# Hybrid decoder layer on one core: the first product in four row pieces and the front in a pinned order

## The chip, the cores and the metric

The kernel runs on one core of one Trainium2 chip. The metric is the device time of one execution in microseconds (us), from several runs of the same program; lower is better. The core has five engines that work side by side: PE (TensorE, matmuls and transposes), DVE (VectorE), ACT (ScalarE), POOL (GpSimd) and SP (SyncE, which here only issues loads). Each runs its own list of instructions in order and waits on the others by semaphores. SP, ACT and POOL also issue DMA transfers, each from its own queue.

## The reference

One decoder layer for 512 tokens of width 1024: a token mixer that adds attention with compressed, selected and windowed keys to a gated recurrence, then a mixture of 16 experts, then a gated per-layer embedding. The change touches the very beginning, where the input is normalised and multiplied with the first columns of `w_in`:

```python
def rmsnorm(x, g):
    xf = x.astype(jnp.float32)
    y = xf * lax.rsqrt(jnp.mean(xf * xf, axis=-1, keepdims=True) + EPS)
    return (y * g.astype(jnp.float32)).astype(x.dtype)
...
        h = rmsnorm(x, g_mix[i])
        z = h @ w_in[i]
        (q_a, kc_a, vc_a, ks_a, vs_a, kw_a, vw_a, gate_a, qk_b, v_b, o_b, if_b, merge) = jnp.split(z, offs, axis=-1)
        nsa_q = partial_rope(q_a.reshape(b, s, NSA_HEADS, NSA_HD), cos, sin)
        k_cmp = partial_rope(kc_a.reshape(b, s, NSA_KV, NSA_HD), cos, sin)
        k_sel = partial_rope(ks_a.reshape(b, s, NSA_KV, NSA_HD), cos, sin)
...
def compress_blocks(tok_g, w1, w2, pe):
...
    blk = tok_g[:, :, idx] + pe
    flat = blk.reshape(b, g, n_cmp, CMP_LEN * d)
    return jax.nn.gelu(flat @ w1) @ w2
```

Columns 0 to 511 of `z` are the queries, 512 to 639 the keys and 640 to 767 the values that are compressed (`kc_a`, `vc_a`), 768 to 1023 keys and values of the selected branch, 1024 to 1279 those of the window. `w_ck1` and `w_cv1` are the two `w1` of the compression, 2048 rows of 256 columns each; `w_ck2`, `w_cv2` the two `w2`.

## The kernel before

**Numbers in two parts.** Every 32-bit factor is split into a hi (rounded to the matmul's format) and a low (the value less its hi), and each product is three matmuls: hi by hi, low by hi, hi by low. For a weight the class `Stream` does this piece by piece: `_load` issues the load of a raw piece on SP (line 77; pool `WR`, four buffers), `_split` makes the hi on ACT (line 103) and the low on DVE (line 106) or on POOL (line 108) from column `pool_from` on. A piece is 128 partitions by 1024 numbers or somewhat less. `get(key)` gives a piece's two parts, loading and splitting in the order of the list.

**Order of the first products.** `ORDER` lists them: `z2` and `z3` are columns 512 to 767 and 768 to 1023, each in two pieces of 256 columns by half of the rows; `z4` is three pieces of 288 columns (1024 to 1303 and eight gate columns), `c0` and `c1` are four pieces each of `w_ck1` and `w_cv1`, and `z0`, `z1` the queries. `z1_mm` and `tok_mm` (matmuls on line 271) run a `z` piece for the four blocks of 128 tokens; `cmp_mm` (line 589) a `c` piece. `z1_out` turns a finished product into what later stages read, partly in generators that `begin` and `advance` call between the matmuls of later pieces.

**The front**, from line 299 on: x is loaded in four blocks (block 0 in two halves, by SP and ACT), and for each block ACT squares and sums it (lines 364 and 390), DVE makes the scale factor (`rstd`, from line 217; `rstd_cols` for blocks 2 and 3 together, from line 231), DVE multiplies it with the factor and the gain (line 372), PE transposes it in eight pieces (line 376), ACT makes the hi `hTh` (line 383) and DVE the low `hTl` (line 385). The gain row is spread over 128 partitions by two matmuls with a row of ones into `gmb` (line 320). Fourteen transposes of an identity, `keep_warm`, are issued there too (line 264). `tok_mm_late` (line 282) runs z2's product for block 0 in an order fit to when its parts come. `angles` (lines 321 to 351) makes the tables of sine and cosine from the positions. Seven small loads fill `rows` (lines 398 to 401), which PE transposes to `cols` (lines 438 to 440). What is not tied by `issue_after` (`after`) is put in order by a scheduler from the data dependences.

**Behind the front.** `finish_c2` transposes the rotated keys (`zt`) and the values (line 526) into `TT`; `cmp_in` adds the position terms into `tb` (line 580) and makes `bhl`, hi (line 581) and low (line 582), which all `c` matmuls read. `w2s` is loaded on POOL (lines 566 and 567) and copied to `w2d` on DVE (line 569). For z3 and z4, `v` (line 547) is the low of the values; it is the last to read an accumulator. The accumulators are in three `mm` and two `S` tiles of PSUM, and transposes go to two `tp`.

## Time and profile before

| | us |
|---|---|
| three runs: median (lowest to highest) | 709.09 (708.98 to 711.17) |
| the profiled execution, its own time | 711.02 |
| its span | 709.3 |
| around the span | 1.72 |
| PE busy, share of the span | 684.3, 96% |
| DVE busy, share of the span | 563.2, 79% |
| ACT busy, share of the span | 436.0, 61% |
| POOL busy, share of the span | 130.4, 18% |

The profile is of one execution, whose own time stands 1.93 above the median of the three runs. Times in it count from the start of the span. An instruction is named by its line, engine and operation, and then by what it writes and reads: `mm<-whWS,hTl` is a matmul into the tile `mm` of a weight's hi by the low of the normalised input. "Idle before" is how long the engine stood before it, and what ended that. Matmuls overlap, so the pace of PE is read from the distance between two starts. "PEclk" is the TensorE clock that was granted, where 1.00 is full speed.

### The profile page before, as it was taken

How to read it: one execution, taken by the hardware profiler on the slowest of the kernel's cores; microseconds unless marked ns; L12 is line 12 of the kernel's file. 1: busy time of each engine (PE TensorE's matmuls, PEld its weight loads, DVE VectorE, ACT ScalarE, POOL GpSimd, SP SyncE). 2: the span in 40 equal slices, each digit the busy share in tenths (PEclk: the TensorE clock that was granted, in tenths of full speed). 3: DMA queues.
4: the chain of work that ended last, by engine and by line, in shares of the span. 5: the costliest groups of instructions: out<-in, count | busy, mean ns of one | idle time of the engine just before them, and what ended most of it. 6: DMA issues, size and time to landing. Idle time of an engine off the chain costs nothing.

```text
span 709.3 us, 11568 instructions
## 1 busy us (share of the span) xinstructions
PE 684.3 (96%) x3913; PEld 584.6 (82%) x3913; DVE 563.2 (79%) x1427; ACT 436.0 (61%) x848; POOL 130.4 (18%) x184
## 2 busy tenths in 40 slices
PE   7989989999999999999999999999999999999995
PEld 5989976889999998888888888876788888887784
DVE  5877989888777758888884673668999999986986
ACT  6447746576666666665553332326999999986642
POOL 5010023333334220000000001222222222110000
PEclk9999999999999999999999999999999999999998
DMA  8424551222121212332219438944999999607511
GB/s 267 124 73 140 167 140 32 85 65 61 31 60 30 61 31 64 87 79 71 83 38 354 146 119 266 375 154 157 388 394 362 355 329 365 245 31 269 191 63 60
DMA packets 83152, 113.72 MB, mean 160 GB/s; under 512 B 9553, under 2 KB 52129, under 8 KB 83090
## 3 DMA queue, kind: packets, MB, share of 16 engines
...
## 4 chain that ended last, share of the span: by engine, by line
PE 79%; DVE 8%; DMA 6%; ACT 4%; issue 2%; POOL 1%; ACTq 0%; POOLq 0%; DVEq 0%
PE mm L945 12%; PE S L1476 11%; PE mm L271 10%; PE mm L1648 6%; PE mm L1501 6%; PE mm L1117 6%; PE mm L768 3%; PE mm L1281 3%; PE S L271 2%; PE tp L862 2%; DMA wr<-in_w_re 2%; PE S L841 2%; PE tp L1462 2%; DVE wlWS L106 1%; ACT whWS L103 1%
## 5 line engine op out<-in xcount | busy, mean ns | idle before, releaser
L106 DVE TENSOR_TENSOR wlWS<-rawWR,whWS 128x1024 fp32r<-128x1024 f32 (+2 forms) x78 | 89.5, 1153 | 28.6 <-ACT whWS L103 27.5
L103 ACT ACTIVATE whWS<-rawWR 128x1024 fp32r<-128x1024 f32 (+2 forms) x79 | 82.3, 1050 | 43.0 <-PE S L271 8.5
L106 DVE TENSOR_TENSOR wlWS<-rawWE,whWS 128x1024 fp32r<-128x1024 f32 x58 | 69.1, 1221 | 3.7 <-ACT whWS L103 2.4
L103 ACT ACTIVATE whWS<-rawWE 128x1024 fp32r<-128x1024 f32 x58 | 60.6, 1071 | 5.1 <-PE S L1476 4.5
L271 PE MATMUL mm<-whWS,hTl 128*128 128x256 f32 (+1 forms) x200 | 59.3, 296 | 1.4 <-DVE hTl L385 1.4
L271 PE MATMUL mm<-wlWS,hTh 128*128 128x256 f32 (+1 forms) x200 | 59.1, 296 | 0.0
L271 PE MATMUL mm<-whWS,hTh 128*128 128x256 f32 (+1 forms) x200 | 59.1, 296 | 0.0
L945 PE MATMUL mm<-hTh,whWS 128*128 128x512 f32 x128 | 50.3, 393 | 0.0
L945 PE MATMUL mm<-hTh,wlWS 128*128 128x512 f32 x128 | 50.0, 391 | 0.0
L945 PE MATMUL mm<-hTl,whWS 128*128 128x512 f32 x128 | 50.0, 391 | 0.0
L852 POOL TENSOR_SCALAR pr<-pr,sm 128x128 f32<-128x128 f32 (+3 forms) x64 | 35.2, 564 | 78.1 <-DVE sm L850 36.4
L1476 PE MATMUL S<-whWS,tgh 128*128 128x512 f32 x120 | 48.6, 405 | 0.0
L1476 PE MATMUL S<-wlWS,tgh 128*128 128x512 f32 x120 | 47.8, 398 | 0.1
L1476 PE MATMUL S<-whWS,tgl 128*128 128x512 f32 x120 | 47.3, 394 | 0.0
L846 ACT ACTIVATE pr<-pr,sm 128x128 f32<-128x128 f32 (+3 forms) x64 | 35.4, 555 | 16.9 <-DVE sm L844 16.8
L271 PEld LDWEIGHTS mm<-whWS,hTl 128*128 128x128 f32 x200 | 38.6, 193 | 1.7 <-DVE hTl L385 1.6
L271 PEld LDWEIGHTS mm<-wlWS,hTh 128*128 128x128 f32 x200 | 38.6, 193 | 0.0
L271 PEld LDWEIGHTS mm<-whWS,hTh 128*128 128x128 f32 x200 | 38.5, 193 | 0.1
L108 POOL TENSOR_TENSOR wlWS<-rawWR,whWS 128x384 fp32r<-128x384 f32 (+1 forms) x17 | 24.8, 1460 | 72.4 <-ACT whWS L103 67.5
L865 ACT ACTIVATE ph<-tp 128x512 fp32r<-128x512 f32 (+1 forms) x48 | 25.1, 523 | 20.4 <-PE tp L862 20.1
L842 DVE CUSTOM_DVE_ANT_0 pr<-S,strip 128x128 f32<-128x128 f32 (+3 forms) x64 | 29.3, 485 | 3.9 <-PE S L841 3.4
...
## 6 DMA issues: line engine op xcount, KB each, us to landing
rawWE<-in_w_e SPq DMA_DIRECT2D x59, 512.0 KB, 9.9
rawWR<-in_w_in SPq DMA_DIRECT2D x40, 512.0 KB, 3.9
mT<-in_w_e SPq DMA_DIRECT2D x22, 512.0 KB, 12.6
rawWR<-in_w_e SPq DMA_DIRECT2D x13, 512.0 KB, 10.4
rawWR<-in_w_out SPq DMA_DIRECT2D x8, 512.0 KB, 4.3
yy<-y_dram SPq DMA_DIRECT2D x8, 512.0 KB, 5.4
rawWR<-in_w_ck SPq DMA_DIRECT2D x4, 512.0 KB, 3.9
rawWR<-in_w_cv SPq DMA_DIRECT2D x4, 512.0 KB, 5.4
```

What stands on the lines that cost most here:

```text
L103: self.last_hi = self.nc.scalar.activation(h[:, :n], flat, AF.Copy)
L106: self.last = self.nc.vector.tensor_tensor(l[:, :c], flat[:, :c], h[:, :c].bitcast(F32), OP.subtract)
L271: T.matmul(dst[b], a[:, kk, b * P:(b + 1) * P], w[:, kk - k0, :n], start=(kk == 0 and i == 0 and b % share == 0), stop=(kk == NK - 1 and i ...
L842: V.tensor_tensor_reduce(pr[:, hh, :n], s_[:, :n], strip[:, 512 - q0:640], 0.125, -3.0e38, OP.add, OP.max, sm[:, 0, hh:hh + 1])
L846: A.activation(pr[:, hh, :n], pr[:, hh, :n], AF.Exp, bias=sm[:, 1, hh:hh + 1], accum_out=sm[:, 2, hh:hh + 1])
L852: G.tensor_scalar(pr[:, hh, :n], pr[:, hh, :n], sm[:, 3, hh:hh + 1], 1.0, op0=OP.mult, op1=OP.mult)
L865: A.activation(ph[:, :nj], tp[:, :nj], AF.Copy)
L945: T.matmul(ps, w[:, k], a[:, k], start=(k == 0 and i == 0), stop=(k == NK - 1 and i == 2))
L1117: T.matmul(ps, w[:, k, f * P:(f + 1) * P], a[:, k], start=(k == 0 and i == 0), stop=(k == 3 and i == 2))
L1476: T.matmul(ps, a[:, 2 * m + k], w[:, k], start=(m == 0 and k == 0 and i == 0), stop=(m == 3 and k == 1 and i == 2))
L1501: T.matmul(acc[c], a[:, k], w[:, 0, c * 512:(c + 1) * 512], start=(k == 0 and i == 0), stop=(k == 1 and i == 2))
L1648: T.matmul(acc, a[:, k], w[:, 0, lo:hi], start=(k == 0 and i == 0), stop=(k == NK - 1 and i == 2))
```

## The change

Columns 512 to 1023 become one product of 512 columns, in four pieces of 256 rows each (`zz`, m = 0 to 3), whose hi and low have a pool of their own (`W0`, four pairs). `zz_mm` runs two k-tiles of a block and some of the three terms, into four accumulators `accz`, one for each block of tokens. The orders of all engines inside the front are pinned by `in_order`, which ties every instruction to the one before it on its engine, in the order of the code:

- all four lows, and the lows of the first two z4 pieces, go to POOL (`pool_from` = 0);
- ten keep-warm transposes stand ahead of the gain matmuls, and these write `mm` and `o`;
- the gain row is loaded by SP in second place, the positions by ACT, and the b_if row, which ACT loaded at the start, comes last of eight small loads on POOL, behind the four lows;
- the positions are cast on POOL and copied from PSUM on ACT; `angles` is in two parts;
- of block 0's squares, the first half is ACT's, the second a `scalar_tensor_tensor` of DVE with a sum;
- z4's first two pieces are fetched inside the front, with accumulators `mm`, `mm`, `mm`, `S`;
- `finish_c2` and z3's outputs are begun ahead of the list, one block pair after the other, and two memsets on POOL stay behind the front.

The diff, cut to what the prediction speaks of:

```diff
-N_WARM = 14
+N_WARM = 10
-ORDER = "z2 z2 z3 z3 z4 z4 c0 z4 c0 c0 z0 c0 z0 c1 z1 c1 z1 c1 c1".split()
+ORDER = "z4 z4 c0 z4 c0 c0 z0 c0 z0 c1 z1 c1 z1 c1 c1".split()
...
+    for m in range(4):
+        st.add(("zz", m), [(0, 512, wall[:, 2 * m:2 * m + 2, 512:1024])], [P, 2, 512], first[0], split_from("W0"))
...
+    def in_order():
...
+            if i.engine in last:
+                tc.add_manual_dep(i, last[i.engine].name, mybir.DependencyInfo(
+                    mybir.DependencyClass.NoSync, mybir.DependencyReason.DATA), reason="in_order")
+            last[i.engine] = i
...
+    def zz_mm(b, m, terms):
+
+        wh, wl = zw[m]
         for i in terms:
             a, w = ((hTh, wh), (hTl, wh), (hTh, wl))[i]
+            for kk in range(2):
+                last = T.matmul(accz[b], a[:, 2 * m + kk, b * P:(b + 1) * P], w[:, kk], start=(m == 0 and i == 0 and kk == 0),
+                                stop=(m == 3 and i == 2 and kk == 1), skip_group_check=True)
+        return last
...
+        st.pool_from = st.split_ahead = 0
+        with in_order():
+            for b in range(NB):
+                t = sp.tile([P, D], F32, name="xs", bufs=NB)
+                if b == 0:
+                    nc.sync.dma_start(t[:, 0:512], x[0, 0:P, 0:512])
+                    A.dma_start(t[:, 512:D], x[0, 0:P, 512:D])
+                    nc.sync.dma_start(grow, g_mix)
+                    A.dma_start(posr, positions[0].rearrange("(a b) -> a b", b=P))
+                else:
+                    nc.sync.dma_start(t, x[0, b * P:(b + 1) * P])
+                xs.append(t)
+                if b < 2:
+                    st._load()
+                    st._load()
...
+            G.tensor_copy(posf, posr)
+            keep_warm(N_WARM)
+
+            gmb = [PM.tile([P, 512], F32, name="mm"), PO.tile([P, 512], F32, name="o")]
+            for c in range(2):
+                T.matmul(gmb[c], ones, grow[:, c * 512:(c + 1) * 512], start=True, stop=True)
+            tpp = PA.tile([P, 512], F32, name="tp")
+            T.transpose(tpp[:, :NB], posf, ident[:NB, :NB])
+            junk0 = [sp.tile([P, 512], F32, name="junk0", bufs=2) for _ in range(2)]
+            A.activation(junk0[0], xs[0][:, 0:512], AF.Square, accum_out=ss[:, 0:1])
+            V.scalar_tensor_tensor(junk0[1], xs[0][:, 512:D], 1.0, xs[0][:, 512:D], op0=OP.mult, op1=OP.mult,
+                                   accum_out=ss[:, 1:2])
+            A.activation(pos, tpp[:, :NB], AF.Copy)
+            V.tensor_tensor(ss[:, 0:1], ss[:, 0:1], ss[:, 1:2], OP.add)
+            rstd(rst[:, 0:1], ss[:, 0:1], sp)
+            for m in range(2):
+                zw.append(st.get(("zz", m)))
+            scaled(0)
+            ps = turned(0)
+            angles_1()
+            square(1)
+            highs(0, ps)
+            rstd(rst[:, 1:2], ss[:, 1:2], sp)
+            lows(0, ps)
+            for m in range(2, 4):
+                zw.append(st.get(("zz", m)))
+            for m, i in ((0, 0), (1, 0), (0, 2), (1, 2), (0, 1), (1, 1), (2, 0), (2, 1), (2, 2), (3, 0), (3, 1)):
+                zz_mm(0, m, (i,))
+            scaled(1)
+            ps = turned(1)
+            zz_mm(0, 3, (2,))
+            square(2)
+            highs(1, ps)
+            square(3)
+            lows(1, ps)
+            rstd_cols(rst[:, 2:4], ss[:, 2:4], sp, 2)
+            scaled(2)
+            scaled(3)
...
+            last_g = nc.gpsimd.dma_start(bif, bass.AP(tensor=b_if.tensor, offset=b_if.offset, ap=[[0, P], [1, 8]]))
+            z4w = [st.get(("z", 4, 0))]
...
-    bif = const.tile([P, 8], F32, name="bif")
-    A.dma_start(bif, bass.AP(tensor=b_if.tensor, offset=b_if.offset, ap=[[0, P], [1, 8]]))
```

`scaled`, `turned`, `highs` and `lows` are the four steps of a block (multiply on DVE, eight transposes on PE, hi on ACT, low on DVE); `turned` is on line 347 of the changed kernel, `zz_mm` on 304.

What the pinned order moves is read from the two programs' lists of instructions, with the line numbers of each kernel.

**ACT, from the first square to block 0's highs.** `junk` is the square, `whWS` and `whW_176`, `whW_183`, `whW_222`, `whW_228` are the hi parts of weight pieces, `pos` the copy of the transposed positions. Before:

```order
5 L390 ACTIVATE junk_136,ss<-xs 128x512
6 L390 ACTIVATE junk_138,ss<-xs 128x512
7 L103 ACTIVATE whWS<-rawWR 128x1024
8 L364 ACTIVATE junk,ss<-xs 128x1024
9 L383 ACTIVATE hTh<-tp 128x4x128 x2
10 L97 ACTIVATE whWS<-rawWR 128x1024
```

With the change:

```order
4 L411 ACTIVATE junk_161,ss<-xs 128x512
5 L414 ACTIVATE pos<-tp 128x4
6 L103 ACTIVATE whW_176<-rawWR 128x1024
7 L103 ACTIVATE whW_183<-rawWR 128x1024
8 L337 ACTIVATE junk,ss<-xs 128x1024
9 L355 ACTIVATE hTh<-tp 128x4x128 x2
10 L103 ACTIVATE whW_222<-rawWR 128x1024
11 L103 ACTIVATE whW_228<-rawWR 128x1024
```

The second half of the square is gone, the copy of `pos` stands ahead of the first hi, two hi stand ahead of block 1's square, and two more come between block 0's highs and the next square.

**POOL, around the small loads.** `wlWS` and `wlW_...` are low parts of weight pieces. Before:

```order
13 L257 AFFINE_SELECT cany<-cany 128x1
14 L108 TENSOR_TENSOR wlWS<-rawWR,whWS 128x1024
15 L398 DMA rows<-in_g_ple 8x128
16 L398 DMA rows<-in_b_conv 8x128
17 L398 DMA rows<-in_g_hn 4x128
18 L398 DMA rows<-in_g_ffn 8x128
19 L399 DMA rows<-in_w_conv 32x128
20 L400 DMA rows<-in_pe_ck 16x128
21 L401 DMA rows<-in_pe_cv 16x128
22 L461 MEMSET strip 128x640
23 L470 MEMSET vcm 128x1024
```

With the change:

```order
14 L108 TENSOR_TENSOR wlW_177<-rawWR,whW_176 128x1024
15 L108 TENSOR_TENSOR wlW_184<-rawWR,whW_183 128x1024
16 L108 TENSOR_TENSOR wlW_223<-rawWR,whW_222 128x1024
17 L108 TENSOR_TENSOR wlW_229<-rawWR,whW_228 128x1024
18 L441 DMA rows<-in_g_ple 8x128
19 L441 DMA rows<-in_b_conv 8x128
20 L441 DMA rows<-in_g_hn 4x128
21 L441 DMA rows<-in_g_ffn 8x128
22 L442 DMA rows<-in_w_conv 32x128
23 L443 DMA rows<-in_pe_ck 16x128
24 L444 DMA rows<-in_pe_cv 16x128
25 L445 DMA bif<-in_b_if 128x8
```

Three more whole lows stand ahead of the loads of `rows`, the load of `bif` is behind them, and two lows of z4 pieces come ahead of the rest.

**DVE, around the copy of `w2d`.** `v_425` and `v_454` are the values of the selected branch (z3), `zt` and `kz` the rotated keys. Before:

```order
67 L482 TENSOR_TENSOR zt<-rope_a,rope_b 128x2x2x16
68 L569 COPY w2d<-w2s 128x256
69 L106 TENSOR_TENSOR wlWS<-rawWR,whWS 128x1024
70 L547 TENSOR_TENSOR v_425<-S,v_425 128x2x64
71 L478 TENSOR_TENSOR rope_a<-kz,trig 128x2x2x8
72 L479 TENSOR_TENSOR rope_a<-kz,trig 128x2x2x8
73 L547 TENSOR_TENSOR v_425<-S,v_425 128x2x64
```

With the change:

```order
67 L510 TENSOR_TENSOR rope_a<-zt,trig 128x2x2x8
68 L511 TENSOR_TENSOR rope_a<-zt,trig 128x2x2x8
69 L514 TENSOR_TENSOR kz<-rope_a,rope_b 128x4x16
70 L601 COPY w2d<-w2s 128x256
71 L512 TENSOR_TENSOR rope_b<-zt,trig 128x2x2x8
72 L513 TENSOR_TENSOR rope_b<-zt,trig 128x2x2x8
73 L579 TENSOR_TENSOR v_454<-S,v_454 128x2x64
74 L584 TENSOR_TENSOR qs<-kz,qs 128x2x2x64
75 L514 TENSOR_TENSOR zt<-rope_a,rope_b 128x2x2x16
76 L579 TENSOR_TENSOR v_454<-S,v_454 128x2x64
```

The copy of `w2d` stood behind both rotations of `zt` and ahead of a weight's low; now it stands between two halves of the second rotation, ahead of the `v_454` that read the accumulator `S`.

## Rows read from the trace of the kernel before

**Rows 1.** The page, busy time of each engine over the whole span.

```profile
PE 684.3 (96%) x3913; PEld 584.6 (82%) x3913; DVE 563.2 (79%) x1427; ACT 436.0 (61%) x848; POOL 130.4 (18%) x184
```

**Rows 2.** Chain of waits, 0 to 110 us: start us, us, what.

```profile
34.23 4.42 DMA w2s<-in_w_ck
...
45.41 2.02 DVE tb L580 x2
```

**Rows 3.** PE's timeline, 0 to 23 us: start us, us, engine, line, operation.

```profile
4.44 3.75 PE L320 MATMUL S<-grow,ones 1*128 1x512 f32 x4 [4.44 <-DMA grow<-in_g_mix]
8.12 3.25 PE L264 MATMUL o<-ident 128*128 128x128 f32 x14
...
15.23 1.03 PE L376 MATMUL tp<-ident,xs 128*128 128x128 f32 x8
...
18.51 0.38 PE L271 MATMUL mm<-whWS,hTl 128*128 128x256 f32 x1 [1.40 <-DVE hTl L385]
```

**Rows 4.** PE's timeline, 40.5 to 52 us.

```profile
41.01 1.03 PE L526 MATMUL tp<-ident,zt 128*128 128x128 f32 x8
...
47.90 0.37 PE L271 MATMUL S<-whWS,hTh 128*128 128x288 f32 x1 [2.00 <-DVE v L547]
48.11 0.29 PE L271 MATMUL S<-whWS,hTl 128*128 128x288 f32 x1
48.24 0.30 PE L271 MATMUL S<-wlWS,hTh 128*128 128x288 f32 x1
...
49.23 0.44 PE L271 MATMUL S<-wlWS,hTh 128*128 128x288 f32 x1
49.47 0.44 PE L271 MATMUL mm<-wlWS,hTh 128*128 128x288 f32 x1
```

**Rows 5.** One window: stretch and us, busy by engine, PEclk, DMA share, GB/s.

```profile
50.00:52.00 2.00, 2.00 (x10) 2.00 (x10) 2.00 (x3) 0.52 (x1) 0.00 (x0) 0.50 0.00 0
```

**Rows 6.** PE's timeline at 68 us.

```profile
68.00 0.28 PE L589 MATMUL o<-wlWS,bhl 128*128 128x256 f32 x1
68.12 0.28 PE L589 MATMUL o<-whWS,bhl 128*128 128x256 f32 x1
```

**Rows 7.** Chain of waits, 255 to 330 us: matmuls of 512 columns.

```profile
270.21 2.74 PE mm L945 x12
```

**Rows 8.** ACT's timeline and queue, 0 to 23 us.

```profile
1.81 0.36 ACTq L695 DMA_DIRECT2D bif<-in_b_if  x1
...
4.20 0.63 ACT L390 ACTIVATE junk<-xs 128x512 f32<-128x512 f32 x1 [0.71 <-DMA xs<-in_x]
...
5.72 1.06 ACT L103 ACTIVATE whWS<-rawWR 128x1024 fp32r<-128x1024 f32 x1
```

**Rows 9.** DMA issues of 0 to 3 us: tile, queue, count, KB each, us to landing.

```profile
xs<-in_x SPq DMA_DIRECT2D x2, 512.0 KB, 7.7
...
posr<-in_positions POOLq DMA_DIRECT2D x1, 2.0 KB, 6.9
```

**Rows 10.** POOL's timeline, 0 to 102 us.

```profile
6.86 2.35 POOL L108 TENSOR_TENSOR wlWS<-rawWR,whWS 128x1024 fp32r<-128x1024 f32 x1 [4.17 <-ACT whWS L103]
9.17 0.56 POOL L398 DMA_DIRECT2D rows<-in_g_ple  x1
...
90.59 2.62 POOL L108 TENSOR_TENSOR wlWS<-rawWR,whWS 128x384 fp32r<-128x384 f32 x2 [36.52 <-ACT whWS L103]
```

**Rows 11.** DVE's timeline, 0 to 101 us.

```profile
7.72 1.41 DVE L372 SCALAR_TENSOR_TENSOR xs<-xs,rst,S 128x512 f32<-128x512 f32 x2
...
91.28 1.05 DVE L478 TENSOR_TENSOR rope_a<-zt,trig 128x64 f32<-128x64 f32 x1
...
93.21 0.21 DVE L480 TENSOR_TENSOR rope_b<-zt,trig 128x64 f32<-128x64 f32 x1
```

**Rows 12.** DVE's timeline, 43 to 50 us.

```profile
43.51 0.75 DVE L534 COPY TT<-tp 64x256 f32<-64x256 f32 x2
...
44.61 0.77 DVE L534 COPY TT<-tp 64x256 f32<-64x256 f32 x2
...
48.59 1.19 DVE L582 TENSOR_TENSOR bhl<-tb,bhl 128x992 fp32r<-128x992 f32 x1 [0.17 <-ACT bhl L581]
```

**Rows 13.** The low on POOL, all of line 108: ns shortest, middle, longest.

```profile
L108 POOL TENSOR_TENSOR wlWS<-rawWR,whWS x17: 997/1642/2352, 6.9 to 228.3; 128x384 fp32r<-128x384 f32 x16, 128x1024 fp32r<-128x1024 f32 x1
```

More of the change, by code (lines that the diff above doesn't have):

```diff
@@ L263, in keep_warm @@
         for _ in range(n):
-            T.transpose(warm[:, 0:P], ident, ident)
+            last = T.transpose(warm[:, 0:P], ident, ident)
+        return last
     def tok_mm_steps(dst, k0, k1, wh, wl, n, share, blocks=range(NB)):
@@ L316, in tile_hybrid @@
[L316 to L332 removed]
+        posf = sp.tile([NB, P], F32, name="posf")
@@ new lines, in scaled, with turned, part @@
+        def scaled(b):
+            for c in range(2):
+                sl = slice(c * 512, (c + 1) * 512)
+                V.scalar_tensor_tensor(xs[b][:, sl], xs[b][:, sl], rst[:, b:b + 1], gmb[c], op0=OP.mult, op1=OP.mult)
+        def turned(b):
+            out_ = [PA.tile([P, 4, P], F32, name="tp") for _ in range(2)]
+            for k in range(8):
+                T.transpose(out_[k // 4][:, k % 4], xs[b][:, k * P:(k + 1) * P], ident)
+            return out_
+        def part(b, c):
+            return tuple(t[:, 4 * c:4 * c + 4, b * P:(b + 1) * P] for t in (hTh, hTl))
@@ L333, in angles, with highs, lows, angles_1 @@
+        def highs(b, ps):
+            for c in range(2):
+                last = A.activation(part(b, c)[0], ps[c], AF.Copy)
+            return last
+        def lows(b, ps):
+            for c in range(2):
+                hh, hl = part(b, c)
+                last = V.tensor_tensor(hl, ps[c], hh.bitcast(F32), OP.subtract)
+            return last
+        def angles_1():
             V.tensor_tensor(ang, inv[:, None, :].to_broadcast([P, NB, 8]), pos[:, :, None].to_broadcast([P, NB, 8]), OP.mult)
-            red = sp.tile([P, 2, NB * 8], F32, name="red")
@@ L571, in tile_hybrid @@
     bhl = zp.tile([P, 16, P], F32R, name="bhl", bufs=1)
-    G.memset(bhl.bitcast(F32), 0.0)
+    with after(last_g):
+        G.memset(bhl.bitcast(F32), 0.0)
     blks = {}
```

212 lines of the change are left out of this document (77 added, 135 removed).

## Prediction

> **What bounds the kernel now.** Read first the engine totals: PE is busy 96% of the span [rows 1], so time is won only where PE idles, runs slowly or does fewer columns; every edit lies in the first 70 us. Then the chain of waits from 0 to 110 us: it hangs on the load of w2s and, later, on `tb` [rows 2], and behind `tb` a `v` of VectorE ends the 2.00 us for which PE stands before 47.90 [rows 4]. Then PE's timeline: the first matmuls, for the gain, wait 4.44 us for the gain row; 14 keep-warm transposes need 3.25 us, 0.23 each, eight transposes at 15.23 need 1.03, 0.13 each [rows 3], so PE's first work runs at about half its later pace, though the granted clock of that stretch reads 1.00. After the 2.00 us of idling it is granted less: 0.50 in 50 to 52 us, the lower of its levels, 1.2 GHz [rows 5]; the pitch of 288-column matmuls goes from 0.13 us (48.11, 48.24) to 0.24 (49.23, 49.47) [rows 4]. From the second matmul of the fourth c0 piece, at 68.00 [rows 6], PE's order is the same in both kernels. I call that place X, and E the end of the product for columns 512 to 1023, 41.01 before, where the transposes of zt follow [rows 4]. The forecast is the time of X after the change.
>
> **Fewer matmuls.** Removed are 192 matmuls of 256 columns, added 96 of 512. The old pitch is 0.12 us (two rows from 68.00) [rows 6]: 192 x 0.12 = 23.0. The pitch of 512 columns stands in a later stage, twelve in 2.74 us, 0.228 each [rows 7]: 96 x 0.228 = 21.9. Gain 1.1 us, all on PE's path. The 32 transposes stay; four fewer keep-warms lie before the first data.
>
> **When block 0 can start.** The gain row goes from ACT's queue to second place on SP's, issued at about the same time, so it lands near 4.4 again; keep-warm goes ahead of the gain matmuls, which take 3.75 us [rows 3], till 8.1. ScalarE now copies `pos` before the first hi; `pos` needs the position transpose, which stands behind the gain matmuls on PE. So hi 0 starts not at 5.72 [rows 8] but at about 8.45, and behind it wait hi 1, square 1 and the highs of block 0. With 1.06 for a hi of 1024 columns [rows 8], and the same for a square or for two highs, which have as many: hi 0 to 9.5, hi 1 to 10.5, square 1 to 11.6 (xs 1, now behind three loads, some 7.7 us after its issue at 2.6 [rows 9], lands near 10.3), highs to 12.6. PE's first product matmul starts at 12.6. Moving half the first square to VectorE gives 0.73 us less to the first scale factor, and it is worth nothing: the second scaled half needs the second gain matmul at 8.1. Its cover is that wait; if the gain came sooner, the 0.73 would count. The b_if load removes 0.36 us from ACT's queue at 1.81, where ACT waits for x until 4.20 [rows 8]: nothing. On POOL it is one of eight issues of at most 0.56 us [rows 10].
>
> **Four lows on POOL in a row.** Before, one low of 1024 columns ran there in 2.35 us [rows 10], the second on VectorE. Now: 9.5 + 4 x 2.35 = 18.9 for the last. Block 0's last term needs it, after which T0, its end, is 18.9 + 2 x 0.228 = 19.3. VectorE's work beside them is priced at its usual duration: two scaled halves took 0.70 each beside the low of 6.86 [rows 10, 11]. Without the lows it would be 12.6 + 24 x 0.228 + 8 x 0.13 = 19.1, so POOL costs 0.2. Then 72 x 0.228 + 16 x 0.13 = 18.5, and 0.6 for block 1's start and the scale factors of blocks 2 and 3 (estimate from the 1.40 us that PE waited at 18.51 before [rows 3], of which the pinned order hides part). E = 19.3 + 18.5 + 0.6 = 38.4 if PE keeps pace. It stands idle between 8.3 and 12.6 except for eight transposes, so I add 0.8 for matmuls of block 0 at the slow pitch. The bounds of that are 0 and 2.2 (all ten matmuls that come before low 2 at twice the pitch). **E = 39.2**, 1.8 earlier than 41.01.
>
> The Trainium skill, page "SBUF — State Buffer", section "SBUF: two separate sides", says that GpSimd and VectorE share a pair of ports as an exclusive lock, held for a whole instruction: a VectorE operation with two SBUF inputs stands still while a GpSimd one reads SBUF. The trace agrees: at 91.28 `rope_a` took 1.05 us beside two POOL lows, `rope_b` of the same size 0.21 when they were over, but the scaled halves, one input of which is in PSUM, took 0.70 each beside the low of 6.86 [rows 10, 11]. By that lock the sum would stay as it is: by my times VectorE's work beside the four lows is rstd 1 (single inputs) and lows and scaled halves from PSUM.
>
> **What starts at E.** The rows' load, eight DMA issues, moved behind the four lows on POOL (18.9 to 23.4) and land by 30.3 even at the 6.9 us that the position row took on that queue [rows 9], before E; then z4's two lows. The w2s load on POOL can start only after the `rows` transpose, as its tile lies over the front's; that transpose now comes at E, where it came well before. Before, w2s was issued at 34.23 and took 4.42 us [rows 2]: it now lands at E + 4.7. VectorE's w2d copy waits for it, and what is queued behind it is the `v` that frees z4's fourth accumulator: PE reaches that after the `rows` transpose and 27 matmuls at 0.133, E + 4.3 with the small waits between, and the low parts behind w2d release it at E + 5.5: **1.2 us** new. PE's transposes of zt now come after the first two pieces of z4, 72 matmuls or 9.5 us: E + 10.9. Behind them ACT and VectorE make one more c0 hi and low (till E + 13.0), then four TT copies (0.75 and 0.77 for two [rows 12]) till 14.9, two tb (2.02 [rows 2]) till 16.9, the bhl hi and its low (1.19 [rows 12]; the hi about as long) till E + 19.4. PE is through z4 and at c0 at E + 16.1, and only four z0 matmuls stand between: **2.9 us** of waiting, then 0.5 for a low of z0. Before, from E to X, it was 68.00 - 41.01 = 27.0, of which 2.17 were waits and 1.7 the slow pitch (14 x 0.11, with the edges), so 23.1 of work. Now 23.1 + 1.2 + 2.9 + 0.5 = 27.7, and, as PE idles for longer than the 2.00 us after which it fell before, I add a fall of 1.2 (ten 256-column matmuls at twice 0.12): 28.9.
>
> **Sum.** X = 39.2 + 28.9 = 68.1 against 68.00: **the gain in front is given back at c0.** Own time 711.02 + 0.1, and as the profiled execution stands 1.93 above the median of the runs (709.09), the time is **709.2 us**. About 0.3%, 2.1 us, is what a measurement of this kernel can tell: faster is under 707.0, slower over 711.2.
>
> **Rival 1, faster: the fall and the slow start don't come.** If the ten keep-warms bring PE to full pace before the gain matmuls, these take half, 1.9 us; `pos` and hi 0 come 1.8 earlier, low 3 ends at 17.1, but square 1 and its data hold the highs near 12, so T0 is 18.4 and E = 37.5; and without the fall at c0 X = 37.5 + 27.7 = 65.2, 2.8 less: 706.4. With the low end of c0's waits (bhl ready 1 us sooner) 705.4. For it: keep-warm work stands in front. Against it: it ends before the gain row lands.
>
> **Rival 2, slower: POOL's lows are the bound.** L108's durations on POOL run from 997 ns to 1642 in the middle, for 384 columns all but once [rows 13], a factor of 1.65, beside a busy VectorE. With four lows at 2.35 x 1.5 = 3.5 the last ends at 23.5, T0 = 24.0, E + 4.7: 713.9. It decides from about 22 us for the last low, 0.8 more each. For it: VectorE is busy beside all four. Against: the one 1024-column low ran beside VectorE's scaled halves and still took 2.35, the longest on record only by its size.
>
> **Rival 3, slower: VectorE stands behind a low.** As `rope_a` did at 91.28 [rows 11], the first product of the angles would wait for low 0 on POOL, up to 2.35, should hi 0 end before 8.9; rstd 1 and the lows of block 0 are queued behind it, and PE waits for these: T0 + 2.3, 711.5. By my times it misses the low by 0.5 us. (The Trainium skill's lock on the page "SBUF — State Buffer" says the same of it.)
>
> **Rival 4: w2s lands late.** The position row took 6.9 us on POOL's queue [rows 9] against 4.42 for w2s: up to 2.5 more in PE's wait at z4: 711.7.
>
> **Chances.** Forecast, within 0.3%: 0.44. Rival 1 and lesser forms of it: 0.32. Rival 2: 0.11, rival 3: 0.05, rival 4 and sums of small waits: 0.08, slower together 0.24. The range reaches from the low end of rival 1, 705.2, to 712.8, which leaves out most of rival 2; the forecast alone holds from 707 to 711.2.
>
> **What would show it.** Right: product matmuls begin near 12.6; POOL's lows stand in a row at 2.35 each and the last ends near 19; E near 39; the w2s load begins at E; PE waits before z4's fourth accumulator, and again for bhl at c0; X near 68. Wrong: lows over 3 us; gain matmuls of half the time; w2s issued well ahead of E; or a fall of the granted clock elsewhere. Any difference that stands after X but not at X would overthrow the whole method.

## The result and the profile after

The changed kernel is slower: 715.0 us median (714.43 to 716.62, 5 runs) against 709.09 before, a ratio of 1.0071, 95% interval 1.0043 to 1.0099. The forecast was 709.2, in a range of 705.2 to 712.8.

| us | before | forecast | after |
|---|---|---|---|
| median of the runs | 709.09 | 709.2 | 715.0 |
| own time of the profiled execution | 711.02 | 711.1 | 715.42 |
| span | 709.3 | | 713.7 |
| E, end of columns 512 to 1023 on PE | 41.01 | 39.2 | 41.54 |
| X, second matmul of the fourth c0 piece | 68.00 | 68.1 | 72.11 |
| from E to X | 27.0 | 28.9 | 30.6 |

The span grew by 4.4 us and X moved by 4.1, so nearly all of it happens ahead of X, where the forecast looked for it. Against before, E is 0.5 later and the way from E to X 3.6 longer; the forecast had wanted E 1.8 earlier.

PE's timeline of the changed kernel, from its start to block 2 (start us, us, engine, line, operation, idle before in brackets), answers to [rows 3]:

```profile
1.53 2.40 PE L284 MATMUL o<-ident 128*128 128x128 f32 x10 [1.53 <-POOL ident masks.py:199]
4.36 2.04 PE L407 MATMUL mm<-grow,ones 1*128 1x512 f32 x2 [0.42 <-DMA grow<-in_g_mix]
6.20 1.91 PE L407 MATMUL o<-grow,ones 1*128 1x512 f32 x2
...
11.82 2.08 PE L304 MATMUL mm<-whW,hTh 128*128 128x512 f32 x4 [1.69 <-ACT hTh L355]
...
15.40 1.26 PE L304 MATMUL mm<-whW,hTl 128*128 128x512 f32 x4
...
20.12 0.67 PE L304 MATMUL mm<-whW,hTh 128*128 128x512 f32 x2
...
23.62 0.61 PE L304 MATMUL mm<-whW,hTl 128*128 128x512 f32 x2
24.07 0.61 PE L304 MATMUL mm<-wlW,hTh 128*128 128x512 f32 x2
26.83 1.33 PE L347 MATMUL tp<-ident,xs 128*128 128x128 f32 x8 [2.14 <-issue]
```

Keep-warm now comes first, the two gain matmuls still take 3.75 us from 4.36 to about 8.1 (two and two in the rows), and the first product matmul starts at 11.82. Block 0 ends with the two matmuls ahead of 20.12, so T0 is 20.1, as forecast. Then PE stands: 2.14 us ahead of the transposes of block 2 at 26.83. The word "issue" there means that the profile names nothing that PE waited for. POOL's and VectorE's timelines show what it was:

```profile
9.38 9.38 POOL L108 TENSOR_TENSOR wlW<-rawWR,whW 128x1024 fp32r<-128x1024 f32 x4 [4.00 <-ACT whW L103]
...
22.48 0.58 POOL L445 DMA_DIRECT2D bif<-in_b_if  x1
23.08 2.06 POOL L108 TENSOR_TENSOR wlWS<-rawWR,whWS 128x864 fp32r<-128x864 f32 x1
...
42.09 0.83 POOL L598 DMA_DIRECT2D w2s<-in_w_ck  x1 [3.39 <-PE tp L468]
...
43.65 1.83 POOL L605 MEMSET bhl<- 128x2048 f32 x1
```

```profile
9.46 2.33 DVE L370 TENSOR_SCALAR kk<-kk 128x64 f32<-128x64 f32 x1
...
22.24 0.16 DVE L237 TENSOR_TENSOR rs_n<-rs_n 128x2 f32<-128x2 f32 x1
...
22.43 2.73 DVE L239 SCALAR_TENSOR_TENSOR rs_n<-rs_n 128x2 f32<-128x2 f32 x1
25.20 0.16 DVE L240 SCALAR_TENSOR_TENSOR rs_n<-rs_n 128x2 f32<-128x2 f32 x1
...
25.98 0.75 DVE L342 SCALAR_TENSOR_TENSOR xs<-xs,rst,mm 128x512 f32<-128x512 f32 x1
...
44.55 1.07 DVE L601 COPY w2d<-w2s 128x256 f32<-128x256 f32 x1
```

The four lows stand in a row on POOL, 9.38 in all or 2.35 each, to 18.76, as forecast. Then come the eight small loads, and at 23.08 the low of z4's first piece, for 2.06 us. On VectorE the scale factors of blocks 2 and 3 are under way: the instruction of line 237 took 0.16, that of line 239, of the same kind and size as line 240 (0.16), is listed with 2.73 and ends at 25.16, when POOL's low does (25.14). So `scaled(2)` starts at 25.98 and PE gets its first transposes 0.85 later. It had met the same thing before: line 370 of the angles took 2.33 us beside the first of the four lows.

Behind E, PE's timeline shows three waits, and its place X:

```profile
41.54 0.24 PE L468 MATMUL tp<-ident,rows 92*128 92x92 f32 x1
...
57.50 0.39 PE L292 MATMUL mm<-whWS,hTh 128*128 128x256 f32 x1 [0.49 <-ACT whWS L103]
...
58.69 0.39 PE L292 MATMUL mm<-whWS,hTh 128*128 128x256 f32 x1 [0.68 <-DVE v L579]
...
61.23 0.58 PE L622 MATMUL o<-whWS,bhl 128*128 128x256 f32 x1 [2.03 <-DVE bhl L615]
```

```profile
72.11 0.28 PE L622 MATMUL o<-wlWS,bhl 128*128 128x256 f32 x1
```

The waits are 0.49 for a hi of z0's first piece, 0.68 for `v` and 2.03 for bhl. None stands at z4's fourth accumulator: w2s was issued at 42.09, right after E, but landed in 2.4 us, where 4.42 was the row of before [rows 2], and its copy on VectorE could start at 44.55. The copy itself took 1.07 beside POOL's memset of 43.65. Windows of two microseconds (stretch and us, busy time with counts for PE, its weight loads, DVE, ACT and POOL, then PEclk, DMA share, GB/s) answer to [rows 5]:

```profile
58.00:60.00 2.00, 0.51 (x3) 0.30 (x2) 1.91 (x9) 1.36 (x2) 0.00 (x0) 1.00 0.00 0
60.00:62.00 2.00, 0.78 (x3) 0.78 (x4) 1.94 (x4) 1.96 (x6) 0.00 (x0) 0.54 0.00 0
62.00:64.00 2.00, 2.00 (x12) 2.00 (x11) 1.97 (x10) 1.76 (x3) 0.00 (x0) 0.50 0.00 0
64.00:66.00 2.00, 2.00 (x11) 2.00 (x11) 1.94 (x4) 1.98 (x5) 0.00 (x0) 0.50 0.01 2
66.00:68.00 2.00, 2.00 (x15) 2.00 (x14) 2.00 (x4) 1.42 (x2) 0.00 (x0) 0.76 0.92 256
```

PE did 0.51 us of work in 58 to 60, and from 60 on its granted clock is 0.54 and 0.50, the lower level, until 66 to 68. The 25 matmuls of c0 from 61.23 on take 5.49 us from start to start (the next one starts at 66.72), 0.22 each, where 0.12 is their pace at the full clock: 2.5 us lost.

### The profile page after: what moved, and what is told of

Same layout as the page of the kernel before. It is cut to its first block, busy times and chain, and to the rows that moved or that the text cites. A ratio compares the mean times of both kernels' runs of the same rounds, so it can differ in the third digit from the quotient of the medians.

```text
span 713.7 us, 11358 instructions
## 1 busy us (share of the span) xinstructions
PE 687.4 (96%) x3813; PEld 581.1 (81%) x3813; DVE 565.1 (79%) x1422; ACT 435.1 (61%) x849; POOL 141.7 (20%) x190
## 4 chain that ended last, share of the span: by engine, by line
PE 81%; DVE 7%; DMA 5%; ACT 4%; issue 2%; POOL 1%; ACTq 0%; SPq 0%; POOLq 0%; DVEq 0%
PE S L1509 12%; PE mm L978 12%; PE mm L292 9%; PE mm L1681 6%; PE mm L1534 6%; PE mm L1150 6%; PE mm L801 3%; PE mm L1314 3%; PE tp L895 2%; DMA wr<-in_w_re 2%; PE S L874 2%; PE S L292 2%; PE tp L1495 2%; PE mm L304 2%; PE o L622 1%
## 5 line engine op out<-in xcount | busy, mean ns | idle before, releaser
L106 DVE TENSOR_TENSOR wlWS<-rawWR,whWS 128x1024 fp32r<-128x1024 f32 (+1 forms) x74 | 85.8, 1168 | 30.1 <-ACT whWS L103 29.2
L103 ACT ACTIVATE whWS<-rawWR 128x1024 fp32r<-128x1024 f32 (+1 forms) x76 | 79.0, 1050 | 38.6 <-PE mm L1150 8.6
L292 PE MATMUL mm<-whWS,hTh 128*128 128x256 f32 (+1 forms) x184 | 54.2, 295 | 1.2 <-DVE v L579 0.7
L292 PE MATMUL mm<-whWS,hTl 128*128 128x256 f32 (+1 forms) x184 | 54.2, 294 | 0.0
L292 PE MATMUL mm<-wlWS,hTh 128*128 128x256 f32 (+1 forms) x184 | 54.1, 295 | 0.0
L108 POOL TENSOR_TENSOR wlWS<-rawWR,whWS 128x384 fp32r<-128x384 f32 (+1 forms) x18 | 26.5, 1475 | 58.9 <-ACT whWS L103 54.0
L292 PEld LDWEIGHTS mm<-whWS,hTh 128*128 128x128 f32 x184 | 35.0, 190 | 2.0 <-DVE v L579 1.2
L292 PEld LDWEIGHTS mm<-wlWS,hTh 128*128 128x128 f32 x184 | 35.0, 191 | 0.0
L292 PEld LDWEIGHTS mm<-whWS,hTl 128*128 128x128 f32 x184 | 34.9, 190 | 0.1
```

Of the source, the lines that this page charges most:

```text
L103: self.last_hi = self.nc.scalar.activation(h[:, :n], flat, AF.Copy)
L106: self.last = self.nc.vector.tensor_tensor(l[:, :c], flat[:, :c], h[:, :c].bitcast(F32), OP.subtract)
L108: self.nc.gpsimd.tensor_tensor(l[:, c:n], flat[:, c:], h[:, c:n].bitcast(F32), OP.subtract)
L292: T.matmul(dst[b], a[:, kk, b * P:(b + 1) * P], w[:, kk - k0, :n], start=(kk == 0 and i == 0 and b % share == 0), stop=(kk == NK - 1 and i ...
```

## The experiments

The theory after these readings: two separate losses, **A**, POOL's low that holds VectorE's scale factors, and **B**, PE's wait for bhl with the fall of the granted clock behind it. The rivals were that A's instruction is only listed long, that B's wait has another cause that stays, and that one brings the other about. E is read from PE's timeline as the start of what follows the last matmul of columns 512 to 1023; Y is the last matmul of c0 and c1. Ratios are to the kernel before in the same session, with 95% intervals; its median there was 710.20 (experiments 1 to 4), 709.95 (5 to 8) and 710.33 (9 to 12), so medians of different sessions are compared with that spread in mind. The changed kernel itself ran only in the session of the result; experiments 4 and 8, which equal it in time, stand in for it in theirs. Single profiles of one front differ by up to a microsecond in E (experiments 1 and 12), so medians decide.

| kernel | median us | ratio to before | E | Y |
|---|---|---|---|---|
| before | 709.09 | 1 | 41.01 | 92.04 |
| changed | 715.0 | 1.0071 (1.0043 to 1.0099) | 41.54 | 96.13 |
| 1 gate | 712.76 | 1.0051 (1.0032 to 1.0069) | 39.04 | 92.62 |
| 2 zt early | 717.34 | 1.0103 (1.0073 to 1.0134) | 42.16 | 98.53 |
| 3 gate and zt early | 713.47 | 1.0053 (1.0035 to 1.0072) | 39.84 | 95.01 |
| 4 square on ACT | 715.13 | 1.0076 (1.0055 to 1.0097) | 46.04 | 100.79 |
| 5 gate, pos late | 711.24 | 1.0021 (1.0004 to 1.0037) | 38.60 | 91.97 |
| 6 gate, z0 first | 709.3 | 0.9993 (0.9980 to 1.0007) | 38.84 | 91.42 |
| 7 fill | 712.47 | 1.0031 (1.0015 to 1.0047) | 41.11 | 93.88 |
| 8 b_if at the front | 715.4 | 1.0075 (1.0055 to 1.0096) | 41.94 | 95.53 |
| 9 = 5 with 6 | 707.96 | 0.9966 (0.9948 to 0.9983) | 37.50 | 90.29 |
| 10 = 9, c0 split early | 708.51 | 0.9969 (0.9952 to 0.9986) | 38.69 | 92.24 |
| 11 before, filled | 710.31 | 0.9993 (0.9979 to 1.0007) | 42.9 | 92.60 |
| 12 gate and fill | 710.72 | 1.0000 (0.9985 to 1.0015) | 40.06 | 92.83 |

**1. A gate for POOL's low.**

```diff
             last_g = nc.gpsimd.dma_start(bif, bass.AP(tensor=b_if.tensor, offset=b_if.offset, ap=[[0, P], [1, 8]]))
+            G.tensor_copy(gate, rst[:, 2:4])
             z4w = [st.get(("z", 4, 0))]
```

> A tiny copy of the scale factors of blocks 2 and 3 stands on POOL ahead of z4's first low, so that low cannot start before VectorE has made them. Theory (one scale-factor instruction with two SBUF inputs stood behind that low for 2.7 us, and PE 2.14 us behind it at 24.7): the instruction takes some 0.16, scaled(2) starts near 23.3 instead of 25.98, PE's wait there is under 0.3, the second c0 matmul of the fourth piece (place X) moves from 72.1 to about 70, the time falls by about 2 us. Rival (PE waits there for the data of block 2 or for ScalarE, the instruction is only listed long): the wait stays over 1.5 us and X moves by under 0.7.

VectorE's timeline with the gate, and POOL's low:

```profile
22.39 0.16 DVE L239 SCALAR_TENSOR_TENSOR rs_n<-rs_n 128x2 f32<-128x2 f32 x1
...
23.37 0.75 DVE L343 SCALAR_TENSOR_TENSOR xs<-xs,rst,mm 128x512 f32<-128x512 f32 x1
...
23.55 2.05 POOL L108 TENSOR_TENSOR wlWS<-rawWR,whWS 128x864 fp32r<-128x864 f32 x1
```

Line 239 takes 0.16, `scaled(2)` starts at 23.37 instead of 25.98, and PE has no wait there. E comes at 39.04, 2.5 sooner than in the changed kernel, X at 68.59, 3.5 sooner; the median falls by 2.2, by 2.4 against experiment 4 of the same session. Theory A holds: a low that starts 0.47 us later, behind the scale factors, brings `scaled(2)` 2.6 us forward. The single profiles agree: E lies between 37.50 and 40.06 in all seven with the gate, between 41.11 and 46.04 in all five without. With the gate, E is where the forecast had put it (39.2).

**2. The transposes of zt after one piece of z4.**

```diff
-    begin(f2, WAIT[0])
+    begin(f2, 5)
```

> Only the due time of the transposes of zt is changed, so that they follow z4's first piece instead of the second. Theory (the transposes of zt, placed late by the new order of the list, hold back bhl, PE waits 2.03 us for it and then runs six microseconds at half the granted clock): bhl is ready some 4 us or more sooner, PE has no wait at c0, the granted clock of 58 to 68 us stays near 1.00, X moves from 72.1 to about 66.5 (2.0 of the wait, 0.7 of the wait for v, 2.4 of the slow pitch, and some), the time falls by 4 to 6 us. Rival (the c0 wait only moves to the next late thing, the hi and low of c0 pieces or the w2s load): X moves by under 2.5 us and a wait of over 1 us stands elsewhere before X.

It is not faster: the median is 2.3 us higher, 2.2 above experiment 4 of the same session, with intervals that overlap. The theory as put there falls. bhl is ready at 57.24 instead of 61.23, but the scheduler now puts c0 matmuls among those of z4, and PE stands at other places:

```profile
57.24 0.39 PE L622 MATMUL o<-whWS,bhl 128*128 128x256 f32 x1 [1.63 <-DVE bhl L615]
...
63.52 0.63 PE L589 MATMUL tp<-ident,qs 128*128 128x128 f32 x4 [0.86 <-DVE kll L595]
65.30 0.38 PE L622 MATMUL o<-whWS,bhl 128*128 128x256 f32 x1 [1.15 <-ACT whWS L103]
```

It stands 1.63 for bhl, 0.86 for a copy of z4's keys, 1.15 for the hi of a c0 piece and, at 66.88, 1.20 for a low of z0, and again the granted clock falls (0.55 and 0.50 from 66 us). So bhl coming sooner is worth nothing while the work that was to cover its making is placed behind it.

**3. Both.**

```diff
+            G.tensor_copy(gate, rst[:, 2:4])
...
+    begin(f2, 5)
```

> Both edits together. If the two causes are separate and both lie on PE's path, the gains add: X near 64.5, 7 to 8 us less than the changed kernel, the time about 707 to 708, at or a little under the kernel before. If one hides the other: no more than the larger alone plus 0.7.

713.47: not what was expected for gains that add, since the second has none; against the second alone the gate gives 3.9, against the first alone the early transposes cost 0.7, which the intervals do not tell from nothing.

**4. The half square back on ScalarE.**

```diff
-            V.scalar_tensor_tensor(junk0[1], xs[0][:, 512:D], 1.0, xs[0][:, 512:D], op0=OP.mult, op1=OP.mult,
-                                   accum_out=ss[:, 1:2])
+            A.activation(junk0[1], xs[0][:, 512:D], AF.Square, accum_out=ss[:, 1:2])
```

> The second half of the first square goes back from VectorE to ScalarE, all else as in the changed kernel. Theory (that edit is covered by the wait for the second gain matmul): X within 0.3 of 72.1 and the time within 0.3% of the changed kernel. Rival (the earlier scale factor brings block 0 forward): first product matmul and X later by 0.4 to 0.8 us.

The median is that of the changed kernel (715.13 against 715.0), as the theory has it. Its profiled execution, with a span of 717.8, is the longest of its five (719.51; the others took 714.07 to 715.72). In it POOL's lows start at 9.09 instead of 9.38, 0.3 us sooner, while VectorE's order is the same:

```profile
8.83 0.18 DVE L365 TENSOR_TENSOR ang<-inv,pos 128x32 f32<-128x32 f32 x1
...
9.14 2.35 DVE L368 COPY red<-ang 128x64 f32<-128x64 f32 x1
11.42 2.39 DVE L369 TENSOR_SCALAR kk<-kk 128x32 f32<-128x32 f32 x1
13.84 2.32 DVE L370 TENSOR_SCALAR kk<-kk 128x64 f32<-128x64 f32 x1
16.08 0.14 DVE L219 TENSOR_SCALAR rs_m<-ss 128x1 f32<-128x1 f32 x1
...
27.93 1.94 DVE L240 SCALAR_TENSOR_TENSOR rs_n<-rs_n 128x2 f32<-128x2 f32 x1
```

Three instructions of the angles, each of one input, wait for three of POOL's lows in turn, 7.06 us for what takes 0.55. Then `rstd` for one column runs beside the fourth low at its usual 0.14 to 0.27, from 16.08 on, and the instruction of 27.93 waits for a z4 low like line 239 before. E is 46.04 in that execution.

**5. The copy of the positions behind the first two hi.**

```diff
-            A.activation(pos, tpp[:, :NB], AF.Copy)
...
             for m in range(2):
                 zw.append(st.get(("zz", m)))
+            A.activation(pos, tpp[:, :NB], AF.Copy)
             scaled(0)
...
+            highs(0, ps)
             square(1)
-            highs(0, ps)
-            rstd(rst[:, 1:2], ss[:, 1:2], sp)
             lows(0, ps)
+            rstd(rst[:, 1:2], ss[:, 1:2], sp)
```

> With the gate of the first experiment; besides, the copy of the positions on ScalarE stands behind the first two hi parts instead of ahead of them, and block 0's highs and lows stand ahead of block 1's square and scale factor. Theory (the copy holds the first hi from about 5.5 to 8.25, and with it the chain of four POOL lows): POOL's lows begin about 2 us sooner (near 7.5), the first product matmul about 0.9 sooner (near 10.9), the last low ends near 17, E near 37.5 against 39.0 with the gate alone, the time 1 to 1.5 us less than with the gate alone. Rival (the raw pieces land too late for that, or the highs have no effect since block 0 waits for its lows): E within 0.4 of the gate alone.

ScalarE's timeline shows that the copy was not what held the first hi:

```profile
8.08 1.06 ACT L103 ACTIVATE whW<-rawWR 128x1024 fp32r<-128x1024 f32 x1 [3.31 <-DMA rawWR<-in_w_in]
9.44 1.06 ACT L103 ACTIVATE whW<-rawWR 128x1024 fp32r<-128x1024 f32 x1 [0.29 <-DMA rawWR<-in_w_in]
```

The first raw piece lands at 8.08 and the second at 9.44, so the hi parts wait for loads that stand third and fourth on SP's queue, and POOL's lows begin at 9.22, not near 7.5. E is 38.60, 0.4 sooner than with the gate alone, at the edge of what the rival allowed; the median is 1.5 lower (711.24 against 712.76). That the gain comes from the sooner E alone is not shown, it is larger than the shift.

**6. A whole piece of z0 ahead of c0.**

```diff
+            G.tensor_copy(gate, rst[:, 2:4])
...
-ORDER = "z4 z4 c0 z4 c0 c0 z0 c0 z0 c1 z1 c1 z1 c1 c1".split()
+ORDER = "z4 z4 z4 z0 c0 c0 c0 z0 c0 c1 z1 c1 z1 c1 c1".split()
```

> With the gate; besides, the list puts the first piece of the queries' columns (z0) whole ahead of the first c0 piece, so that PE has 48 matmuls of work (5.8 us) while bhl is made. Theory (what the changed kernel loses behind E is PE's idling for bhl and the fall of the granted clock after it): the wait of 2.0 us for bhl and the stretch at half the granted clock are gone, the distance from E to the last matmul of c0 and c1 falls from 53.6 with the gate alone to about 50, the time falls by 3 to 4 us below the gate alone, to about 709. Rival (the chain of VectorE behind it sets that distance, not PE): the distance falls by under 1.5 us, and new waits stand in front of c0 or c1 pieces.

709.3, 3.5 below the gate alone, as expected. By the distance from E to Y, though, it was the rival's sign that came: it fell by 1.0, not 3.6, and Y came only 1.2 sooner. The two profiles show 1.9 of the 3.5 (711.7 to 709.79): the gate's is the fastest of its five executions, 1.1 under their median, and the one here lies 0.5 over its own. The granted clock reads 1.00 from 42 to 120 us; there is no wait for bhl, but there are two others (PE's waits: us, times, longest):

```profile
PE o L624 <- DVE wlWS L106: 1.4, 1, 1.4
PE tp L643 <- ACT qst L548: 1.4, 1, 1.4
```

**7. Idle transposes in the wait.**

```diff
         A.activation(bhl[:, :, 0:62], tb, AF.Copy)
+        blks[kv] = PO.tile([P, 512], F32, name="o")[:, :256]
+        if kv == 0:
+            for q in range(14):
+                T.transpose(blks[kv][:, 0:P], tb.rearrange("p a b -> p (a b)")[:, 0:P], ident)
         V.tensor_tensor(bhl[:, :, 64:126], tb, bhl[:, :, 0:62].bitcast(F32), OP.subtract)
-        blks[kv] = PO.tile([P, 512], F32, name="o")[:, :256]
```

> The changed kernel with 14 idle transposes on PE in the wait for bhl, tied to tb, so that they run from about 58.4 to 60.2. They do no useful work. Theory (the idling makes the clock fall, and the fall costs some 2.4 us by itself): c0 still starts near 61.2, the granted clock of 60 to 68 us is near 1.00, the last matmul of c0 and c1 comes about 2 us sooner. Rival (the clock falls for another reason): it still shows 0.5 in that stretch and nothing is gained.

PE's timeline, and the windows of the same stretch:

```profile
57.92 1.75 PE L618 MATMUL o<-ident,tb 128*128 128x128 f32 x14 [0.47 <-DVE tb L613]
60.78 0.39 PE L625 MATMUL o<-whWS,bhl 128*128 128x256 f32 x1 [0.77 <-DVE bhl L619]
```

```profile
60.00:62.00 2.00, 1.23 (x11) 1.22 (x11) 1.94 (x3) 1.98 (x5) 0.00 (x0) 1.00 0.00 0
62.00:64.00 2.00, 2.00 (x18) 1.84 (x16) 1.97 (x10) 1.97 (x5) 0.00 (x0) 1.00 0.00 0
64.00:66.00 2.00, 1.56 (x13) 1.52 (x13) 1.94 (x5) 2.00 (x5) 0.00 (x0) 1.00 0.19 19
```

PE still waits for bhl, 0.77 at 60.78, but the granted clock stays at 1.00 and c0 runs at 0.12 per matmul. The median falls by 2.5 with not one useful instruction added, by 2.9 against experiment 8 of the same session; in the profiles the distance from E to Y falls by 1.8 (54.59 to 52.77). It is not the profiled execution alone: each execution is recorded with its mean granted clock, which is 0.995 to 0.997 in the eight of this kernel, 0.991 to 0.994 in the changed kernel's five and 0.992 to 0.995 in experiment 8's four. So the fall costs about as much as the wait of 2.03 itself.

How long the fall lasts is not the same in each execution. Behind the same wait of 2.04 two windows of the gate alone (experiment 1) read:

```profile
60.00:62.00 2.00, 2.00 (x12) 2.00 (x11) 1.97 (x10) 1.97 (x5) 0.00 (x0) 0.51 0.00 0
62.00:64.00 2.00, 2.00 (x13) 2.00 (x13) 1.94 (x5) 2.00 (x4) 0.00 (x0) 0.63 0.22 24
```

From 64 on it is 1.00 again: some 16 matmuls at the lower pace there, and 16 in experiment 8, where the changed kernel's profile has 25. Of the 3.5 us that X came sooner in experiment 1, about 1.0 is this.

**8. The b_if load back at the front.**

```diff
+                    A.dma_start(bif, bass.AP(tensor=b_if.tensor, offset=b_if.offset, ap=[[0, P], [1, 8]]))
...
-            last_g = nc.gpsimd.dma_start(bif, bass.AP(tensor=b_if.tensor, offset=b_if.offset, ap=[[0, P], [1, 8]]))
```

> The changed kernel with the b_if load back on ScalarE's queue at the start, all else as it is. Theory (that edit is worth nothing by itself; POOL's low of z4 starts 0.58 sooner and still holds the scale factors): VectorE's blocked instruction ends near 24.6 instead of 25.2, PE's wait at 24.7 is 1.5 to 2.1, the time within 0.3% of the changed kernel. Rival (the load's issue on POOL, with its 128 descriptors, is itself what blocks VectorE at 22.43): the block is shorter by more than 0.6 us, or gone.

715.4, as the changed kernel. Without the load's issue VectorE is blocked all the same: the instruction of line 240 stands 1.93 us and ends with POOL's low of 23.69 to 25.74.

```profile
23.82 1.93 DVE L240 SCALAR_TENSOR_TENSOR rs_n<-rs_n 128x2 f32<-128x2 f32 x1
```

The block is 0.80 shorter than in the changed kernel, which was to be the rival's sign, and PE's wait is 1.24, under the 1.5 expected; but the scale factors also begin 1.26 later in this run (22.82 instead of 21.56), and E, at 41.94, is no sooner. One thing stays open. In the changed kernel line 239 is listed from 22.43 on, 0.65 before the low, while the load was being issued (22.48 to 23.06); in experiment 7 it is the same with line 240, by 0.58. With the gate, lines 240 to 243 took 0.16 each beside that issue (22.62 to 23.20). So the low holds VectorE, and the issue alone does not; why the hold begins ahead of the low's listed start no run shows.

**9 and 10. Towards a version that beats both.** The ninth is the fifth with the list of the sixth. The tenth also loads and splits the first c0 piece ahead of z4's third:

```diff
-    for o in ORDER:
+    for o in "z4 z4 c0 z4 z0 c0 c0 z0 c0 c1 z1 c1 z1 c1 c1".split():
         c, h = int(o[1]), seen.get(o, 0)
```

> The fifth and sixth experiments together: gate, copy of the positions behind the first hi parts, block 0's highs and lows first, and z0's first piece whole ahead of c0. If their gains add (about 1.5 below the gate alone from the first, 3.5 from the second): the last matmul of c0 and c1 near 90.7, the time 707.5 to 708.5, about 1 us under the kernel before. If the wait for the low of the first c0 piece only grows when E comes sooner: the same as the sixth, about 709.3.

> As the ninth, but the first c0 piece is loaded and split ahead of z4's third piece, in VectorE's idle time, while PE's order stays. Theory (in the sixth PE stood 1.4 us for that piece's low, which VectorE made behind bhl): that wait is gone and the last matmul of c0 and c1 comes 1 to 1.4 us sooner, about 89.5, the time near 707. Rival (the making of bhl itself is as late): the wait goes over to bhl and the gain is under 0.4.

The ninth takes 707.96, ratio 0.9966 (0.9948 to 0.9983): the gains add, and it is faster than the kernel before. The tenth is the same within its interval (0.9969); PE's wait for a c0 low is still 1.4. It is not the first piece's low: in experiments 6, 9 and 10 alike 17 matmuls of c0, two pieces of eight and one, stand ahead of the wait. PE waits for the third piece, which the edit left where it was.

**11. The kernel before with its wait filled.** In z4's first piece 16 transposes of the identity stand between the third and the fourth block:

```diff
+            tok_mm(dst, *K4[h], wh, wl, 288, 1, range(3))
+            idle = PO.tile([P, 512], F32, name="o")
+            with tc.issue_after(tok_last[0].ins):
+                for q in range(16):
+                    done = T.transpose(idle[:, 0:P], ident, ident)
+            with tc.issue_after(done.ins):
+                tok_mm(dst, *K4[h], wh, wl, 288, 1, range(3, 4))
```

> The kernel before with 16 idle transposes on PE in the stretch in which it stands 2.0 us for v (45.9 to 47.9). Theory (there too the fall of the granted clock comes from the idling and costs some 1.5 us): the granted clock of 48 to 52 us reads 1.00, the fourth c0 piece's second matmul moves from 68.0 to about 66.5, the time falls by 1 to 1.7 us. Rival (the kernel before falls in some of its runs only): the profile shows the same, but the median falls by under 0.5 us.

PE's timeline and three windows of it, two in the front and one behind:

```profile
47.40 1.91 PE L499 MATMUL o<-ident 128*128 128x128 f32 x16
49.70 0.37 PE L273 MATMUL S<-whWS,hTh 128*128 128x288 f32 x1 [0.40 <-DVE v L557]
```

```profile
18.00:20.00 2.00, 0.95 (x8) 0.95 (x9) 1.93 (x6) 1.46 (x2) 0.00 (x0) 0.99 0.73 211
20.00:22.00 2.00, 2.00 (x12) 2.00 (x11) 1.56 (x3) 0.07 (x1) 0.00 (x0) 0.50 0.01 4
...
110.00:120.00 10.00, 9.80 (x48) 7.55 (x47) 8.51 (x37) 5.62 (x18) 2.79 (x6) 0.83 0.19 56
```

The wait is filled (0.40 is left of 2.00) and the clock behind it is 1.00, yet the median does not move: 710.31 against 710.33 of the same sessions. The profiled execution has falls elsewhere: 0.50 in 20 to 22, behind the wait for a low of hTl in front (0.95 us of work in 18 to 20), a wait that had no fall behind it in the profile of before (1.00 in 20 to 22), and 0.83 as the mean of 110 to 120. The mean granted clock of each execution speaks for the rival, that the kernel before falls in some of its runs only. Of its 35 beside experiments 9 to 12, the 20 at 0.996 or more took 708.49 to 710.62 us, the six at 0.991 or 0.992 took 712.70 to 713.60; the profiled one, with its fall at 48 us, has 0.994. The filled kernel's twelve spread as widely, 0.992 to 0.997. Where the single executions fall is not shown, since each kernel has one profile.

**12. Gate and fill.**

```diff
+            G.tensor_copy(gate, rst[:, 2:4])
...
+            for q in range(14):
+                T.transpose(blks[kv][:, 0:P], tb.rearrange("p a b -> p (a b)")[:, 0:P], ident)
```

> The changed kernel with the gate of the first experiment and the idle transposes of the seventh. If the collision and the fall of the clock are two separate losses (2.2 and 2.5 us by the medians): about 710.2, the last matmul of c0 and c1 near 90.5, and what is left against the kernel before is the wait for bhl of 2 us. If one brought the other about: no less than 711.8.

710.72: 2.0 below the gate alone, 1.8 below the fill alone, 4.3 below the changed kernel, ratio to before 1.0000 (0.9985 to 1.0015). Y is 92.83, not near 90.5: E came 1.0 later in this profile than in the gate's, and the fall that the fill takes away was the short one there (E to Y 53.58; here 52.77, as with the fill alone). The losses are two, they add, and together they are as large as the slowdown, within 1.1 us either way.

## Why the prediction was wrong

**What held.** The price of 512-column matmuls (two in 0.45 us from 23.62 to 24.07, 0.228 forecast for each); no gain from the b_if load and from the half square (experiments 8 and 4); POOL's lows at 2.35 each beside a busy VectorE, which ends rival 2; the w2s load at E; bhl 19.7 us behind E (forecast 19.4) and 3.2 us of waits around it (2.9 and 0.5), though bhl's own is 2.03, not 2.9. The method held too: what the span lost, it had lost by X. Two numbers were right by luck. T0 came at 20.1, but the first product matmul started at 11.82, not 12.6, and the eight matmuls from there to 15.40 took 0.45 each instead of 0.228, 1.8 us where 0.8 was put. And the first hi did wait until 8.25, but its raw piece landed near 8 as well (experiment 5).

**The step that failed first: "0.6 for block 1's start and the scale factors of blocks 2 and 3", and with it "VectorE's work beside them is priced at its usual duration".** I had a rival for exactly this mechanism, VectorE standing behind a low, and put it at the angles, where it missed the path: there it cost 2.33 us on VectorE and hardly anything on PE (in experiment 8 the same line took 0.20, and E was no sooner). It struck at the other place. POOL's eight loads end at 23.06 and its next low starts at once; the scale factors of blocks 2 and 3 start when their squares are done, at 21.56. The prediction had the loads end at 23.4, but gave the scale factors no time of their own and did not lay the two beside each other, because it asked only for VectorE's work beside the *four* lows. In place of 0.6 the term measured 2.14 for the one wait and some 0.8 for smaller ones: E 41.54, not 39.2. The same wait was 1.23 to 1.99 in the profiles of experiments 2, 4, 7 and 8. The gate brings E back to 39.04.

The rule that I cited from the Trainium skill, page "SBUF — State Buffer", section "SBUF: two separate sides", names two kinds of VectorE operations that a GpSimd one locks out: those with two SBUF inputs, and those in a two-port performance mode. I read the first kind only. The runs agree with both kinds as far as they go: scale-factor instructions of two inputs waited (2.73, 1.94, 1.93 us), and so did copies and scalings of one input on 128x32 and 128x64, each until a low's end (2.32 to 2.39 in experiment 4); one-column `rstd` (0.14 at 16.08 there) and the scaled halves with a PSUM input (0.74 at 14.52 in the changed kernel) did not. In which mode an instruction ran no trace lists.

**The second: "a fall of 1.2 (ten 256-column matmuls at twice 0.12)".** The place and the cause were right, the size was not: 25 matmuls ran at 0.22, 2.5 us, and in experiments 1 and 8, behind the same wait, 16, some 1.5 us by the same pace. The ten were a guess at its length, where the rows of before had the lower pace from 49 to 52 us behind 2.00 us of idling [rows 4, 5], and here PE had idled 0.49, 0.68 and 2.03 us in turn. On the other side stands the wait of 1.2 at z4's fourth accumulator, which did not come because w2s landed in 2.4 us. The rest of E to X is 24.9 us against 23.1. The work is the same in both kernels, 169 matmuls of 256 and 288 columns and as many transposes of zt and qs, so the 1.8 lie in PE's slower starts around its waits and between the groups, which I had not counted.

**The third: the step from the profile to the median.** The forecast took the changed kernel's profile to stand 1.93 above its median, as before's did. It stands 0.4 above. Of the miss of 5.8 us, 4.3 are in the profile and 1.5 are here. The losses of the changed kernel are in all its runs (mean granted clock 0.991 to 0.994); what lifted the one execution of before, 0.994, was not in its median: most of its runs in the last session have 0.996 or more (experiment 11).

**Rivals.** Rival 1's price for "no fall" was 1.2, and the fill shows 2.5; its other half, gain matmuls at full pace, did not come (3.75 us as before). Rival 3 was right in mechanism and in sign (711.5) and wrong in place; rival 4 went the other way.
